# A list scheduler that reckons with a later landing of the compressed branch's first weights

## The chip, the cores and the metric

One core of a Trainium2 chip. The metric is the device time of one execution in microseconds (us), smaller is better. TensorE (PE) multiplies, VectorE (DVE) and ScalarE (ACT) do the elementwise work, GpSimd (POOL) a little of it, and SyncE (SP) issues all transfers from one queue.

## What is computed

A decoder layer on 512 tokens of width 1024 in float32. One normalised input goes through one projection into two attention mixers and their gates:

```python
h = rms_norm(x, norm_w[l])
proj = h @ w_in[l]
(q_a, k_a, v_a, z_a, q_b, kc, vc, ksl, vsl, kwn, vwn, gate_b, z_b, gate_m) = jnp.split(proj, split_points, axis=-1)
...
k_cmp = rms_norm(compress(heads(kc), cmp_pos_k[l], cmp_w1_k[l], cmp_w2_k[l]), k_norm_cmp[l])
v_cmp = compress(heads(vc), cmp_pos_v[l], cmp_w1_v[l], cmp_w2_v[l])
```

Mixer A (8 heads, "MoBA") and mixer B (8 heads, "NSA") are softmax attentions with a bias by distance. Mixer B has a third branch over compressed keys and values: `compress` takes windows of 32 tokens, 16 apart, adds a position term, and multiplies each window (2048 numbers) by a first weight (2048 x 256), applies gelu and multiplies by a second weight (256 x 64). Both mixers' outputs are gated with silu, projected to 1024, merged by sigmoid gates, projected once more and added to x.

## The kernel before, in words

**Products in pieces.** A float32 weight tile (128x512) is loaded into a raw buffer `wr`. ScalarE rounds it to the high part (`wh`, for the compressed branch `vh`), DVE subtracts that from the raw tile to get the low part (`wl`, `vl`), and PE multiplies both. The rounding is the cast of L402, the subtraction L412; the method that emits both is `Stream.split`. The raw buffers (`NRAW` = 6) are shared by all weights and come back first in, first out: the n-th load of a raw tile waits until the subtraction six raw tiles earlier is done. A stream of weights loads its next tile right behind the subtraction of an earlier one (`w.load`, called at the end of `split`'s chain).

**Two streams.** `W` holds the weights of the projections and of the end, in the trace `in_wtok`, `in_wchan` and `in_wbr`. `W1` holds the first weights of `compress`, in the trace `in_w`: 16 tiles, eight for K and then eight for V. `compress_h` takes them one by one: four matmuls per tile into `hps` (L940), two with the high part and two with the low part; after the eighth tile ScalarE copies `hps` to `hs` (L947), PE turns it round (`pu`, L952), and gelu and the second weight follow.

**Attention.** Per head: scores `sps` (PE, L1094), bias `T` and the maximum (DVE, L1114), exponential (ACT, L1125) and its factor (L1127, L1128), probabilities in two float16 halves `sb` (ACT L1132, DVE L1136), transposes of these from SP's queue (`dst`, L245), and the product with the values (`O`, PE, L1168). Two heads share one run of 24 such products; there are twelve runs, four for mixer A and eight for mixer B.

**What sets the order.** Every engine's instructions are put in order by a list scheduler that runs in the kernel's own Python. A piece of work is a `Chain`: steps with an engine and a cost in ns. Chains stand in a heap by the time at which their next step may begin; the step with the earliest time is emitted next on its engine, and `free[engine]`, the engine's time in the scheduler's books, moves on by its cost. PE's streams of work (scores, projections, compression, values) are generators that ask when their operand is ready and are taken by turns. A load's time comes from `dma` (L235): its issue, 1000 ns, the bytes and 1700 ns more. This landing time `t` is what a `split` chain starts with, if it is later than the scheduler's present time `now[0]`. Nothing on the chip reads these times; they decide only where an instruction stands in its engine's queue. An engine runs its queue in that order, and each instruction waits for its own operands.

Of the kernel before, what the change touches and what calls it, by code (L numbers as in the profile page):

```python
# [67 lines left out]
XQ = 1200  # L68
XW = 1700.0
XG = 400.0  # L70


QA, KA_, VA, ZA, QB, KC, VC, KSL, VSL, KWN, VWN, GB, ZB, GM = (
# [35 lines left out]
def hybrid_kernel(ctx: ExitStack, tc: tile.TileContext, x, x0, xT, wtok, wchan, gains, w1,  # L109
# [21 lines left out]
    now = [0.0]  # L131
# [14 lines left out]
    def ca(n):  # L146
        return 93 + 0.834 * n
# [13 lines left out]
    def either(n):  # L161
        return {"d": cd(n)}
# [173 lines left out]
    class Stream:  # L336
# [48 lines left out]
        def split(w, upto):  # L385
            for i in range(w.next, min(upto, len(w.tiles))):
                w.next = i + 1
                if isinstance(w.tiles[i], Sum):
                    if i not in w.chain:
                        w.split_sum(i)  # L390
                    continue
                while i not in w.raw:
                    w.load()
                w.ahead -= 1
                n, *squares = w.tiles[i][1:]
                (raw, t), hi, lo = w.raw.pop(i), w.mk_hi()[:, :n], w.mk_lo()[:, :n]
                w.out[i] = hi, lo
                c = w.chain[i] = Chain(max(now[0], t))

                def f(e, hi=hi, raw=raw):  # L400
                    if e is nc.scalar:
                        e.copy(hi, raw)  # L402
                    else:
                        e.tensor_scalar(hi, raw, 1.0, 1.0, op0=ALU.mult, op1=ALU.mult)
                c.do({"D": 205 + 0.54 * n} if w.first and not i else {"A": ca(n)}, f).mark((w, 0, i))
                if squares:
                    d = Chain(held=True)
                    c.call(lambda c=c, d=d: d.start(c.t))
                for o, m, g, acc, fn in squares:
                    d.do({"A": 190 + 0.834 * m}, lambda e, z=hi[:, o:o + m], y=R.bitcast(mybir.dt.bfloat16)[:, :m] if m > 256 else junk, g=g, acc=acc: e.activation(  # L410
                        y, z.bitcast(F32), AF.Square, scale=g, accum_out=acc)).call(lambda fn=fn, d=d: fn(d.t))
                c.do(either(n), lambda e, hi=hi, lo=lo, raw=raw: e.tensor_sub(lo, raw, hi.bitcast(F32))).mark((w, 1, i))  # L412
                c.call(w.load)
# [85 lines left out]
    def att(name, dt=F32R):  # L499
        return ap_.tile([P, 512], dt, name=nm(name), tag="a")  # L500
# [49 lines left out]
    def x_rms():  # L550
# [5 lines left out]
        for t in range(NT):  # L556
            nc.tensor.matmul(ps[:, t:t + 1], sq_sum[:, t * P:(t + 1) * P], ones, start=True, stop=True)
            yield 214
            if t < NT - 1:
                ready = now[0] + XG  # L560
                yield lambda: ready
# [98 lines left out]
    W1 = Stream([(w1[kv, q], 512) for kv in range(2) for q in range(8)], 2, lambda: att("vh"), lambda: att("vl"))  # L660
# [238 lines left out]
    def compress_w(kv):  # L899
        st = xws[kv] = []  # L900
        b = {}

        def emit(ps):
            ch = Chain(now[0] + 230)
            for g in range(2):
                for l in range(2):
                    v = lambda z, g=g, l=l: z[g * 64:(g + 1) * 64, :].rearrange("p (j l) -> p l j", l=2)[:, l, :]

                    def f(e, g=g, l=l, v=v):
                        if not g and not l:  # L910
                            b["X"] = alloc("gmt", "X", (P, 2, 256))
                        e.tensor_mul(b["X"][64 * l:64 * l + 64, g, :], v(ps), v(R))  # L912
                    ch.do({"D": 335}, f, ps if g and l else None, None if g or l else "gmt")
            for i8 in range(2):
                XW = att("XW", F32).rearrange("p (i g c) -> p i g c", g=2, c=C32)
                ch.do({"p": 140}, lambda e, XW=XW: e.memset(XW[:, :, :, 31:32], 0.0))
                for g in range(2):
                    ch.do({"d": 550}, lambda e, XW=XW, g=g, i8=i8: e.tensor_tensor(
                        XW[:, :, g, 0:31], b["X"][:, g, :].rearrange("p (c i) -> p i c", i=8)[:, :, i8:i8 + 31],
                        pos[:, kv, 8 * i8:8 * i8 + 8].unsqueeze(2).to_broadcast([P, 8, 31]), op=ALU.add),  # L920
                        (lambda: b["X"]) if i8 and g else None)
                for q in range(2):
                    xs = att("xs")
                    split(ch, xs.rearrange("p (i s c) -> p i s c", s=2, c=64),
                          XW[:, 4 * q:4 * q + 4].rearrange("p i g c -> p i (g c)"))
                    st.extend(xs[:, i * P:(i + 1) * P] for i in range(4))
            ch.mark(f"xw{kv}")
        yield from gemm_chan("kc" if not kv else "vc", emit)
# [75 lines left out]
    def compress_v2(G):  # L1004
        yield room("t")
        ps = psum("t", "pv2")
        for g in range(2):
            for a in range(2):
                nc.tensor.matmul(ps[:, g * 64:(g + 1) * 64], G[:, 2 * a + g].rearrange("p r c -> p (r c)"),
                                 w2t[:, 1, a, :], start=(a == 0), stop=(a == 1))  # L1010
        yield 600
        release(G)
        yield room("nraw")
        vr = alloc("nraw", "vr", (P, 2, DH))
        yield room("nraw")
        vh = alloc("nraw", "vh", (P, 2, 2, DH), F32R)
        vt = att("vz").rearrange("p (g s i d) -> p g s i d", g=2, s=2, i=2)
        vz.extend(vt[:, g] for g in range(2))
        ch = Chain(now[0] + 230)
        ch.do({"D": 200}, lambda e: e.tensor_scalar_mul(vr, ps[:, :P].rearrange("p (g d) -> p g d", g=2), 0.5), ps)  # L1020
        split(ch, vh, vr, vr)
        for g in range(2):
            ch.do({"D": 335}, lambda e, g=g: e.tensor_mul(
                vz[g], vh[:, g].bitcast(F32).unsqueeze(2).to_broadcast([P, 2, 2, DH]),
                hmask.unsqueeze(1).unsqueeze(3).to_broadcast([P, 2, 2, DH])), vh if g else None)
        ch.mark("cmpv")
# [721 lines left out]
```

## Time and profile before

| | |
|---|---|
| median of 3 timed runs | 422.29 us (421.83 to 422.44) |
| the profiled execution | 422.54 us |
| its span in the trace | 420.5 us |
| granted TensorE clock | 1.00 |
| busy: PE, DVE, ACT, POOL | 98%, 85%, 71%, 8% |

A row of a timeline gives the start in us, the duration, the engine, the line, the operation, output<-inputs, the shape and how many; the bracket at its end is the time that the engine stood idle just before, and what ended that. A row of the waits gives who waited, for whom, the total in us, how many times, and the longest. A row of the chain gives a start, a duration and what stood on the chain of work that ended last. Names have their buffer numbers left out.

### The profile page before, as it was taken

Reading aid. Unit: us, or ns where it says so; the run is one execution under the profiler, and the core shown is the slowest. Engines: PE = TensorE matmul, PEld = TensorE weight load, DVE = VectorE, ACT = ScalarE, POOL = GpSimd, SP = SyncE. Lnnn points to the kernel's source line nnn. Section 1 sums busy time; section 2 is a strip of 40 time slices with the busy share of each in tenths; the row PEclk is TensorE's granted clock in tenths of the full one; section 3 lists DMA queues with packets and bytes.
Section 4 is the critical chain, followed back from the end, with each engine's and each line's share of the span. In section 5 each row is a group of like instructions: output and inputs, shape, how many; then the busy total and the mean of one; then the engine's idle time right before and its main releaser. Section 6 shows DMA issues by size and latency. Waiting matters only on the chain.

```text
span 420.5 us, 7307 instructions
## 1 busy us (share of the span) xinstructions
PE 411.8 (98%) x2235; PEld 322.0 (77%) x2235; DVE 356.3 (85%) x933; ACT 297.9 (71%) x793; POOL 35.1 (8%) x37
## 2 busy tenths in 40 slices
PE   9999998999998999999999999999999999999996
PEld 7877875778976677897766777666777888888885
DVE  5967969999899987778999997899956967698993
ACT  7996748997797988727988897898943433445620
POOL 0015100123210033200000000000000000000000
PEclk9999999999999999999999999999999999999999
DMA  8951785688969988750878778889799597251232
GB/s 278 311 190 49 129 271 140 137 183 214 264 201 232 195 163 194 218 153 12 147 168 196 150 161 200 167 195 160 145 162 348 175 374 278 79 180 44 56 143 100
DMA packets 116693, 75.30 MB, mean 179 GB/s; under 512 B 89072, under 2 KB 92016, under 8 KB 116656
## 3 DMA queue, kind: packets, MB, share of 16 engines
q1 hardware_dynamic: 116656, 74.86, 70.5%
q8 instruction: 17, 0.28, 0.3%
q14 instruction: 20, 0.16, 0.1%
HBM read 51.11 MB, written 2.75 MB: 128 GB/s over the span
## 4 chain that ended last, share of the span: by engine, by line
PE 54%; DVE 23%; DMA 9%; ACT 5%; issue 5%; SPq 1%; POOL 1%; DVEq 0%; ACTq 0%; POOLq 0%
PE pgc L437 21%; PE pbr L437 9%; PE po L437 9%; PE pgt L437 8%; DMA wr<-in_wtok 5%; DVE sb L1114 4%; DVE wl L412 4%; DVE sb L1136 4%; DMA wr<-in_w 3%; PE O L1168 3%; PE sps L1094 3%; ACT wh L402 2%; DVE vl L412 1%; SPq L238 1%; DMA T<-rtab 1%
## 5 line engine op out<-in xcount | busy, mean ns | idle before, releaser
L437 PE MATMUL pgc<-hh,wh 128*128 128x512 f32 x208 | 87.1, 419 | 0.0
L412 DVE TENSOR_TENSOR wl<-wr,wh 128x512 fp32r<-128x512 f32 (+1 forms) x112 | 73.1, 669 | 11.8 <-ACT wh L402 11.6
L437 PE MATMUL pgc<-hh,wl 128*128 128x512 f32 x208 | 81.5, 392 | 0.0
L437 PE MATMUL pgc<-hl,wh 128*128 128x512 f32 x208 | 81.2, 390 | 0.0
L402 ACT CAST wh<-wr 128x512 fp32r<-128x512 f32 (+1 forms) x111 | 64.0, 599 | 11.2 <-DMA wr<-in_wtok 5.6
L1125 ACT ACTIVATE sb<-sb,sst 128x256 f32<-128x256 f32 (+3 forms) x96 | 53.2, 554 | 10.5 <-DVE sst L1114 10.2
L437 PE MATMUL pgt<-wh,hh 128*128 128x512 f32 (+2 forms) x160 | 58.3, 364 | 0.1
L437 PE MATMUL pgt<-wl,hh 128*128 128x512 f32 (+2 forms) x160 | 56.1, 351 | 0.5 <-DVE wl L412 0.4
L437 PE MATMUL pgt<-wh,hl 128*128 128x512 f32 (+2 forms) x160 | 55.8, 349 | 0.0
L1136 DVE SCALAR_TENSOR_TENSOR sb<-sb,sst 128x256 f16<-128x256 f32 (+3 forms) x96 | 51.1, 542 | 4.2 <-ACT sb L1132 3.9
L1114 DVE CUSTOM_DVE_ANT_0 sb<-sps,T,gst 128x512 f32<-128x512 f32 (+3 forms) x96 | 51.2, 541 | 3.5 <-PE sps L1094 1.6
L1132 ACT ACTIVATE sb<-sb,sst 128x256 f16<-128x256 f32 (+3 forms) x96 | 51.4, 552 | 4.0 <-DVE sst L1128 3.7
L437 PEld LDWEIGHTS pgc<-hh,wh 128*128 128x128 f32 x208 | 39.1, 188 | 8.6 <-issue 0.3
L437 PEld LDWEIGHTS pgc<-hh,wl 128*128 128x128 f32 x208 | 39.0, 188 | 8.6
L437 PEld LDWEIGHTS pgc<-hl,wh 128*128 128x128 f32 x208 | 39.2, 189 | 6.5
L1094 PE MATMUL sps<-qkt,qkt 128*128 128x512 f16 (+3 forms) x176 | 38.2, 310 | 1.6 <-DVE sst L1114 1.4
L489 POOL TENSOR_TENSOR nr<-nss,mhalf 128x8 f32<-128x8 f32 (+1 forms) x16 | 29.0, 1819 | 109.4 <-DVE nss L488 47.9
L437 PEld LDWEIGHTS pgt<-wl,hh 128*128 128x128 f32 x160 | 30.1, 188 | 5.5 <-DVE wl L412 1.6
L437 PEld LDWEIGHTS pgt<-wh,hh 128*128 128x128 f32 x160 | 30.2, 189 | 4.3 <-DVE X L912 0.4
L437 PEld LDWEIGHTS pgt<-wh,hl 128*128 128x128 f32 x160 | 30.2, 189 | 3.4
L1094 PEld LDWEIGHTS <-qkt 128*128 128x128 f16 x176 | 11.5, 98 | 21.4 <-issue 18.5
L437 PE MATMUL pbr<-yh,wh 128*128 128x512 f32 x64 | 26.4, 413 | 0.0
(229 smaller groups left out, 746.3 us busy)
## 6 DMA issues: line engine op xcount, KB each, us to landing
wr<-in_wchan SPq DMA_DIRECT2D x52, 256.0 KB, 3.8
wr<-in_wtok SPq DMA_DIRECT2D x36, 256.0 KB, 4.0
wq<-in_wout SPq DMA_DIRECT2D x36, 256.0 KB, 3.1
T<-rtab SPq DMA_DIRECT2D x16, 256.0 KB, 4.0
wr<-in_w SPq DMA_DIRECT2D x16, 256.0 KB, 3.7
wr<-in_wbr SPq DMA_DIRECT2D x16, 256.0 KB, 3.1
xr<-in_x SPq DMA_DIRECT2D x8, 256.0 KB, 5.3
x<-in_xT SPq DMA_DIRECT2D x7, 256.0 KB, 5.8
```

What stands on the lines that cost most here:

```text
L238: nc.sync.dma_start(out=dst, in_=src)
L402: e.copy(hi, raw)
L412: c.do(either(n), lambda e, hi=hi, lo=lo, raw=raw: e.tensor_sub(lo, raw, hi.bitcast(F32))).mark((w, 1, i))
L437: nc.tensor.matmul(dst, sts[i][a], mvs[i][b], start=(start and i == a == b == 0), stop=(stop and i == n - 1 and (a, b) == passes[-1]), ski ...
L489: c.do({"p": 700 + 150 * w}, lambda e: e.tensor_tensor(v(dst), v(ss), mhalf[:parts, :w], op=ALU.pow))
L1094: nc.tensor.matmul(sps[:, :n].rearrange("p (t n) -> p t n", n=P), qs, k4[:, x, j, :b + 1], start=not x, stop=bool(x))
L1114: e.tensor_tensor_reduce(z["sb"], sps[:, :L], T[:, S - L:], scale=nrunscale, scalar=3e38, op0=ALU.add, op1=ALU.min, accum_out=st[:, 0, b:b ...
L1125: c.do({"A": 279 + 0.834 * L}, lambda e: e.activation(z["sb"], z["sb"], AF.Exp, bias=st[:, 0, b:b + 1], scale=-1.0, accum_out=st[:, 1, b:b ...
L1132: e.activation(z["pp"][:, :L], z["sb"], AF.Copy, scale=s_)
L1136: c.do({"d": 59 + cd(L)}, lambda e: e.scalar_tensor_tensor(z["pp"][:, L:], z["sb"], s_, z["pp"][:, :L], op0=ALU.mult, op1=ALU.subtract))
L1168: nc.tensor.matmul(out, v[r][kb][:, vi * DH:(vi + 1) * DH], u.moving(kb, pi), start=p.first and kb == vi == pi == 0, stop=p.last and kb == ...
```

## The change

The landing time with which a `split` chain of the stream `W1` starts is put 1000 ns later. The other stream's chains, all costs, buffers and instructions stay as they are. Line numbers behind the new constant are one higher afterwards.

```diff
 XQ = 1200
 XW = 1700.0
 XG = 400.0
+LAND1 = 1000
...
                 n, *squares = w.tiles[i][1:]
                 (raw, t), hi, lo = w.raw.pop(i), w.mk_hi()[:, :n], w.mk_lo()[:, :n]
                 w.out[i] = hi, lo
-                c = w.chain[i] = Chain(max(now[0], t))
+                c = w.chain[i] = Chain(max(now[0], t + (LAND1 if w is W1 else 0)))
```

Counts and kinds of instructions are the same on every engine. PE's order is the same up to about 94 us of the trace and after the last run of attention products apart from what is shown below; between them it differs in many places.

ScalarE, round the copy of K's finished hidden sums `hs`. `vh_1736<-wr_1719` is the cast of V's first tile, `vh_1703` (not shown) that of K's last; `wh` are casts of other weights, `sb` and `sst` belong to the attention, `kb` to its keys. Before:

```order
L402 CAST vh_1736<-wr_1719 128x512
L1125 ACTIVATE sb_1771,sst_1723<-sb_1771,sst_1723 128x256
L1127 ACTIVATE sst_1723<-sst_1723 128x1
L1365 ACTIVATE th_1817<-zs_1660 128x512
L1132 ACTIVATE sb_1676<-sb_1676,sst_1580 128x128
L1125 ACTIVATE sb_1789,sst_1723<-sb_1789,sst_1723 128x128
L1127 ACTIVATE sst_1723<-sst_1723 128x1
L1132 ACTIVATE sb_1730<-sb_1730,sst_1723 128x512
L1033 COPY kb_1550<-kb_1550 128x2x64
L1127 ACTIVATE sst_1723<-sst_1723 128x1
L947 COPY hs_1853<-hps_1130 128x256
```

The same place now, where V's first tile is `vh_1818<-wr_1809`:

```order
L1034 COPY kb_1541<-kb_1541 128x2x64
L1128 ACTIVATE sst_1717<-sst_1717 128x1
L804 CAST kb_1542<-nraw_1559 128x2x64
L948 COPY hs_1863<-hps_1130 128x256
L403 CAST wh_1871<-wr_1663 128x512
L403 CAST wh_1873<-wr_1679 128x512
L403 CAST wh_1875<-wr_1690 128x512
L403 CAST wh_1877<-wr_1708 128x512
L1034 CAST kb_1542<-nraw_1559 128x2x64
L1200 CAST yh_1840<-zs_1654 128x512
L403 CAST vh_1818<-wr_1809 128x512
```

The cast of V's first tile stood ten rows ahead of the copy and stands seven rows behind it. The cast of K's last tile, which stood sixteen rows ahead of the copy, is now twelve rows ahead.

SyncE, the loads of the same tiles. `in_w` are first weights, `in_wtok` other weights, `rtab` the bias, `qkt` and `dst` transposes of the attention's keys and probabilities. Before, from K's last tile (`wr_1697`) on:

```order
L238 DMA wr_1697<-in_w 128x512
L238 DMA wr_1706<-in_wtok 128x512
L245 DMA_TRANSPOSE qkt_1438<-kb_1431 128x8x128
L238 DMA wr_1719<-in_w 128x512
L238 DMA T_1721<-rtab 128x1x512
L238 DMA wr_1742<-in_wtok 128x512
L245 DMA_TRANSPOSE dst_1794<-sb_1585 128x8x128
L245 DMA_TRANSPOSE dst_1794<-sb_1597 128x6x128
```

Now, where K's last tile is `wr_1721` and V's first `wr_1809`:

```order
L239 DMA wr_1690<-in_wtok 128x512
L239 DMA wr_1708<-in_wtok 128x512
L239 DMA T_1715<-rtab 128x1x512
L239 DMA wr_1721<-in_w 128x512
L246 DMA_TRANSPOSE qkt_1431<-kb_1424 128x8x128
L246 DMA_TRANSPOSE dst_1735<-sb_1575 128x8x128
L246 DMA_TRANSPOSE dst_1735<-sb_1587 128x6x128
L239 DMA wr_1809<-in_w 128x512
```

Both loads have moved back; V's first is behind two transposes of probabilities that it stood ahead of.

TensorE, the end of the last run of attention products (L1168, now L1169). `ch` and `vz` are the compressed branch's probabilities and values, `pgc` a projection with the weights `wh` and `wl`, `pbr` the branches' projection. Before:

```order
L1168 LDWEIGHTS vb_2457
L1168 MATMUL O_4200<-dst_4110,vb_2457 64x384
L1304 MATMUL O_4200<-ch_3257,vz_2519 128x512 x2
L437 MATMUL pbr_4331<-yh_3258,wh_4249 128x512
L437 MATMUL pbr_4331<-yl_3259,wh_4249 128x512
```

Now:

```order
L1169 LDWEIGHTS vb_2438
L1169 MATMUL O_4186<-dst_4091,vb_2438 64x384
L1305 MATMUL O_4186<-ch_3337,vz_2558 128x512 x2
L438 MATMUL pgc_4260<-hh,wh_4243 128x512
L438 MATMUL pgc_4260<-hl,wh_4243 128x512
L438 MATMUL pgc_4260<-hh,wl_4244 128x512
```

Twelve matmuls of a `pgc`, of which the first three are shown, ran ahead of this last run and now stand behind it, in front of the `pbr`.

## The prediction, made before the changed kernel ran

> **What bounds the kernel now.** I read the page first, then the windows of 10 us, the waits, the timelines round the largest pauses of TensorE, and the chain. The profiled execution took 422.54 us, 420.5 of it inside the span; 2.0 us lie around the span, and the median of the three timed runs, 422.29, is 0.25 below it, so a change of the span is carried over to the median as it is. The page's totals and its chain:
>
> ```profile
> PE 411.8 (98%) x2235; PEld 322.0 (77%) x2235; DVE 356.3 (85%) x933; ACT 297.9 (71%) x793; POOL 35.1 (8%) x37
> PE 54%; DVE 23%; DMA 9%; ACT 5%; issue 5%; SPq 1%; POOL 1%; DVEq 0%; ACTq 0%; POOLq 0%
> ```
>
> TensorE (PE) works nearly all the time. The change removes no instruction, so it can only win TensorE's pauses. Busy time by stretch (sum of the stretch, then PE, PEld, DVE, ACT, POOL, clock, DMA share, GB/s) shows where they are:
>
> ```profile
> 120.00:130.00 10.00, 10.00 (x52) 7.65 (x51) 10.00 (x33) 7.66 (x23) 0.00 (x0) 1.00 0.97 244
> 130.00:140.00 10.00, 8.53 (x43) 6.22 (x42) 9.63 (x28) 9.78 (x30) 1.01 (x1) 1.00 1.10 223
> 140.00:150.00 10.00, 9.21 (x62) 6.79 (x61) 9.24 (x35) 9.66 (x34) 0.76 (x1) 1.00 0.90 194
> 170.00:180.00 10.00, 9.83 (x74) 9.24 (x73) 8.44 (x23) 6.37 (x17) 2.57 (x2) 1.00 0.69 196
> 220.00:230.00 10.00, 10.00 (x66) 6.97 (x65) 10.00 (x31) 8.64 (x28) 0.00 (x0) 1.00 0.84 168
> 240.00:250.00 10.00, 9.77 (x46) 7.11 (x45) 9.16 (x31) 10.00 (x30) 0.00 (x0) 1.00 0.75 161
> 250.00:300.00 50.00, 50.00 (x299) 34.86 (x298) 44.24 (x139) 44.32 (x132) 0.00 (x0) 1.00 0.85 177
> ```
>
> PE lacks 1.5 us in 130 to 140 and 0.8 in 140 to 150, hardly anything elsewhere, at the full clock. The waits that bear on the change (total, times, longest):
>
> ```profile
> ACT vh L402 <- DMA wr<-in_w: 3.8, 5, 2.3
> DVE vl L412 <- ACT vh L402: 2.5, 5, 0.9
> PE pu L952 <- ACT hs L947: 1.3, 1, 1.3
> PE O L1168 <- DMA dst<-sb: 0.8, 1, 0.8
> PE hps L940 <- DVE vl L412: 0.2, 1, 0.2
> ```
>
> ScalarE (ACT) waits five times for a first weight, 3.8 us in all. The longest one, in ACT's timeline (start, duration, and in brackets the idle time before):
>
> ```profile
> 127.58 0.29 ACT L1033 CAST kb<-nraw 128x128 f16<-128x128 f32 x1
> 130.22 0.62 ACT L402 CAST vh<-wr 128x512 fp32r<-128x512 f32 x1 [2.34 <-DMA wr<-in_w]
> 130.74 0.50 ACT L1125 ACTIVATE sb<-sb,sst 128x256 f32<-128x256 f32 x1
> ...
> 133.53 0.35 ACT L947 COPY hs<-hps 128x256 f32<-128x256 f32 x1
> ```
>
> and TensorE's, for the two pauses:
>
> ```profile
> 132.22 0.40 PE L437 MATMUL pgt<-wl,hh 128*128 128x512 f32 x1
> 133.94 0.66 PE L952 MATMUL pu<-cst,hs 128*128 128x64 f32 x4 [1.32 <-ACT hs L947]
> ...
> 146.34 0.40 PE L437 MATMUL pgt<-wl,hh 128*128 128x512 f32 x1
> 146.67 0.40 PE L1168 MATMUL O<-dst,v 128*64 128x512 f16 x1
> 147.86 1.66 PE L1168 MATMUL O<-dst,v 128*64 128x512 f16 x22 [0.79 <-DMA dst<-sb]
> ...
> 156.94 0.51 PE L940 MATMUL hps<-vh,xs 128*128 128x256 f32 x2
> ```
>
> The cast at 130.22 rounds the first V tile, whose product PE takes up at 156.94, 26 us later. Yet ACT stands in front of it for 2.34 us, and behind it in the queue is the copy of `hs` (K's finished hidden sums) for which PE waits. The matmul of 132.22 should have been followed 0.23 us later (twelve take 2.73 below), so this pause costs 1.5 us; the third attention product (`O`, at 146.67) loses 1.1 in the same way, waiting for a transpose. The chain between them, and what later rows I need:
>
> ```profile
> 125.56 4.64 DMA wr<-in_w
> 130.22 0.63 ACT vh L402
> 145.11 2.71 DMA dst<-sb
> 147.86 1.66 PE O L1168 x19
> 168.47 3.65 DMA wr<-in_w
> 172.13 0.63 ACT vh L402
> 172.78 0.70 DVE vl L412
> 243.47 2.73 PE pgc L437 x12
> ```
>
> **The change part by part.** One number moves the assumed landing of each first weight 1.0 us back; all else is what the list scheduler makes of it.
>
> *The V tile's cast goes behind the copy of hs.* Ten rows ahead of it before, seven behind it now. The 2.34 us no longer stand in front of the copy. What does is K's last tile: its cast, then eleven rows of the same forms as those that ran between 130.22 and 133.53 (3.3 us for ten), which I put at 3.2 us, so the copy starts 3.8 us after that cast starts and is done 0.35 later. On PE's side the cast (0.63) and the subtraction (0.70) come before K's last product, and from there to `pu` the order holds 2.1 us of products: PE arrives 3.5 us after the cast starts, the copy ends at 4.2. So 0.7 of the 1.5 stay: **-0.8**. Bounds: all of it goes (-1.5), or nothing (0), where ACT now waits as long at K's last tile.
>
> *The third attention product.* It now has six more products ahead of it (1.4 us by 2.73 for twelve), and the probabilities that its transposes read come from the ACT queue that stood still. A pause of 1.1 under a cover of 1.4: **-1.1**. Without this cover, if the transposes come later too, 0.
>
> *V's last tile.* 0.3 us of PE (0.2 on the product, the rest on its weight load) goes with the chain of 168.47; the product now has 4 us more work ahead of it: **-0.3**.
>
> *New waits.* K's fourth and last tile are loaded and rounded later in the order; the raw buffers come back first in, first out, so the last tile's load starts when the subtraction six loads earlier is done. A load takes 3.7 us (median) to 4.64:
>
> ```profile
> wr<-in_w SPq DMA_DIRECT2D x16, 256.0 KB, 3.7
> ```
>
> plus the cast's 0.63, and DVE has only about 3.8 us of other work between these two subtractions. DVE then stands for 0.5 to 1.5 us, and PE has two groups of products in hand: I take **+0.3**, bounds 0 and 1.2. [...]
>
> These four give PE 1.9 us by about 180 us.
>
> *What PE is given and has to give back.* From 250 on PE has no pause, so 1.9 us is the gain unless a later product is late. The order puts the last attention product earlier: twelve matmuls that ran ahead of it (2.73 us) now run after it. SyncE's queue (SP) feeds it with transposes, and is full. The last of them in SP's timeline, their landing (count, median from issue), and the product:
>
> ```profile
> 242.51 1.05 SPq L238 DMA_DIRECT2D wr<-in_wchan  x2
> 245.10 9.75 SPq L245 DMA_TRANSPOSE dst<-sb  x7
> ...
> 305.34 8.86 SPq L245 DMA_TRANSPOSE dst<-sb  x6
> ```
>
> ```profile
> dst<-sb SPq DMA_TRANSPOSE x2, 3.0
> ```
>
> ```profile
> 316.43 1.82 PE L1168 MATMUL O<-dst,vb 128*64 128x512 f16 x24
> ```
>
> The last transpose was issued at 313.0 and landed at 316.0: 0.4 us of slack, 0.6 with the first product that doesn't need it. PE would now be there 1.9 + 2.7 = 4.6 us earlier. If the transposes come s earlier, PE waits 4.0 - s. Bounds: s = 4 (SP had gaps ahead of 245.10, the last of them 1.5 us, so its queue can follow), wait 0; s = 0 (DVE is full at 220 to 230 and sets when probabilities come), wait 4.0, the whole gain and 2.1 more. I take s = 2.9: the 1.9 that PE's products for this stage come earlier, and 1.0, an estimate, for a subtraction (0.7) and a few small steps that stand behind, no longer ahead of, the probabilities that filled SP's queue at 245.10. Wait: **+1.1**.
>
> Sum: -0.8 - 1.1 - 0.3 + 0.3 + 1.1 = -0.8 us, so 422.54 becomes 421.7 and the median **421.5**. A measurement of this kernel can tell about 0.2% (0.84 us) from no change, so this case lies on the line between the two.
>
> **The rivals.**
>
> *The transposes don't follow (slower).* At the last attention product everything depends on s; the end moves by 2.1 - s (never below -1.9), so it decides at s = 2.1. For: the chain of the selection scores now has a gate of channel `zs` ahead of it in DVE, which waits for a later PE product, DVE has no idle time at 220 to 230, and SP has none from 245 to 314, so nothing lost before 245 is won back. Against: ahead of these probabilities DVE has less to do, not more. With s between 0 and 1.2 the end is 0.9 to 2.1 later: 423.2 to 424.4, middle **423.8**.
>
> *The wait only changes its place.* ACT waits at K's last tile, whose load now starts late, as long as it did at V's first (2.3), and DVE and PE with it; or the changed loads leave PE's pauses as long in other rows. For: five waits on these loads existed, and a cast further back also loads its successor later, since the next load is started after the subtraction. Against: the one that cost most was a tile not yet needed. PE then keeps -0.3 of the three gains, and the end is **422.0** to 422.5.
>
> *The change doesn't do what it says:* the loads of these weights are issued further back too (two of them now stand behind transposes of 1.2 us each, as the 4.64 us load did), so the casts wait as before. It ends like the rival before, and is counted with it.
>
> *All of it is gained.* The transposes follow fully (s = 4): -1.9, or **420.4**.
>
> **How the numbers follow.** Forecast case (s between 2.1 and 4, end 420.4 to 422.3) 0.54, of which 0.34 lies beyond 0.84 us faster; all gained, with the pause at `hs` gone too, 0.08; the wait moves 0.16, 0.10 of it within 0.2% and 0.06 of it slower (new waits at K's tiles at their upper bound, with nothing gained at 147); the transposes don't follow 0.22, of which 0.20 is over the line. So faster 0.42, same 0.32, slower 0.26. The range runs from 420.2 (all gained and 0.2 more of the pause at `hs`) to 423.6 (s = 0.4); the forecast case alone is 420.4 to 422.3.
>
> **What would show it.** Right: ACT's 2.34 us wait is gone, `hs` is copied within 4 us of the cast of K's last tile and PE's pause at `pu` is 0.5 to 1.0; no pause at the third attention product; a pause of about 1 us at the last one or two of them, with `dst` as what ended it. Wrong: PE pauses by over 2 us in the sum of the last attention products (slower rival), or ACT still waits over 2 us on a first weight ahead of `hs` (the wait moved), or PE's 250 to 300 has a pause of another kind.

## The result, and the profile after

The changed kernel is slower. Eleven executions of each gave a median of 427.0 us against 422.24, a ratio of 1.0111 (95% interval 1.009 to 1.0133). One execution of each (430.44 and 452.72) fell in a slower state and is left out of the ratio, here and below. Its profiled execution took 424.81 us with a span of 422.8, 2.3 more than the 420.5 of before. The page's totals, after:

```profile
PE 412.7 (98%) x2235; PEld 323.3 (76%) x2235; DVE 355.5 (84%) x929; ACT 297.4 (70%) x797; POOL 34.5 (8%) x37
```

TensorE still works nearly all the time, so the 2.3 us must be pauses. The windows of the changed kernel show where (columns as in the prediction: sum, PE, PEld, DVE, ACT, POOL, clock, DMA share, GB/s):

```profile
130.00:140.00 10.00, 9.23 (x45) 6.77 (x44) 9.39 (x24) 10.00 (x31) 0.00 (x0) 1.00 1.00 204
140.00:150.00 10.00, 10.00 (x66) 7.12 (x65) 9.93 (x40) 10.00 (x35) 1.74 (x1) 1.00 1.04 223
160.00:170.00 10.00, 9.63 (x61) 7.03 (x61) 5.58 (x12) 7.63 (x22) 1.47 (x2) 1.00 0.95 216
170.00:180.00 10.00, 9.69 (x78) 9.35 (x78) 8.01 (x17) 6.17 (x13) 1.71 (x2) 1.00 0.88 244
220.00:230.00 10.00, 9.34 (x60) 6.55 (x57) 10.00 (x28) 8.57 (x23) 0.00 (x0) 1.00 1.10 160
260.00:270.00 10.00, 7.69 (x52) 5.33 (x51) 7.89 (x22) 8.02 (x24) 0.00 (x0) 1.00 0.84 175
```

The two pauses that the prediction set out from have shrunk: 130 to 140 lacks 0.77 us instead of 1.47, 140 to 150 nothing instead of 0.79. Three new ones stand behind them: 0.7 us in 160 to 180, where before had 0.2, 0.7 in 220 to 230 and 2.3 in 260 to 270, where before had none. The waits name them:

```profile
ACT vh L403 <- DMA wr<-in_w: 2.8, 1, 2.8
PE sps L1095 <- DVE sst L1115: 2.1, 3, 1.1
PE O L1169 <- DMA dst<-sb: 2.0, 1, 2.0
```

ScalarE waits once for a first weight instead of five times. PE's one wait for a transpose, 0.8 us at the third run of attention products before, is now 2.0 us, and it stands elsewhere:

```profile
134.14 0.66 PE L953 MATMUL pu<-cst,hs 128*128 128x64 f32 x4 [0.58 <-ACT hs L948]
147.75 1.94 PE L1169 MATMUL O<-dst,v 128*64 128x512 f16 x23
169.71 0.51 PE L941 MATMUL hps<-vl,xs 128*128 128x256 f32 x2 [0.22 <-DVE vl L413]
172.07 0.50 PE L941 MATMUL hps<-vl,xs 128*128 128x256 f32 x2 [0.31 <-DVE vl L413]
227.16 0.48 PE L1095 MATMUL sps<-qkt,qkt 128*128 128x384 f16 x2 [0.66 <-DVE sst L1115]
...
262.43 0.39 PE L1093 MATMUL sps<-qkt,qkt 128*128 128x256 f16 x2
264.83 1.89 PE L1169 MATMUL O<-dst,vb 128*64 128x512 f16 x24 [2.00 <-DMA dst<-sb]
```

The row of 264.83 is the eighth of the twelve attention runs. The twelfth, at 316.24, has no wait.

**Why the eighth.** The order puts it nine products (2.0 us) further forward than before, and its last transpose comes later. SyncE's queue, in before (the seven transposes ahead of these rows, from 245.10 on, stand in the prediction) and then in the changed kernel:

```profile
254.90 0.57 SPq L238 DMA_DIRECT2D wr<-in_wbr  x1
255.57 0.55 SPq L238 DMA_DIRECT2D T<-rtab  x1
256.17 0.58 SPq L238 DMA_DIRECT2D wr<-in_wchan  x1
256.84 1.23 SPq L245 DMA_TRANSPOSE dst<-sb  x1
258.12 0.57 SPq L238 DMA_DIRECT2D wr<-in_wchan  x1
258.80 6.46 SPq L245 DMA_TRANSPOSE dst<-sb  x5
```

```profile
245.67 4.49 SPq L246 DMA_TRANSPOSE dst<-sb  x3
250.21 0.57 SPq L239 DMA_DIRECT2D wr<-in_wchan  x1
250.88 5.22 SPq L246 DMA_TRANSPOSE dst<-sb  x4
256.15 0.57 SPq L239 DMA_DIRECT2D wr<-in_wbr  x1
256.82 0.55 SPq L239 DMA_DIRECT2D T<-rtab  x1
257.46 1.22 SPq L246 DMA_TRANSPOSE dst<-sb  x1
258.74 1.04 SPq L239 DMA_DIRECT2D wr<-in_wchan  x2
259.89 6.58 SPq L246 DMA_TRANSPOSE dst<-sb  x5
```

and the changed kernel's chain:

```profile
261.23 3.56 DMA dst<-sb
```

The eighth run needs the second of the last five. It was issued at 260.1 (258.80 and a fifth of 6.46) and is now issued at 261.23, 1.1 later; it landed 3.0 after its issue, at 263.15, and now 3.56 after it, at 264.8. Before, the product stood at 264.53 with 1.4 us to spare; now PE is there at 262.8 and waits.

What this transpose moves had long been ready. DVE finished the probabilities at 256.08 in before and at 256.31 now, with this row:

```profile
255.96 0.35 DVE L1137 SCALAR_TENSOR_TENSOR sb<-sb,sst 128x128 f16<-128x128 f32 x1
```

So the transpose stood behind others in SyncE's queue for 4.9 us. The rows above follow each other with at most 0.1 us between them, from 245.67 on (245.10 in before), with nine transposes ahead of this one in both kernels, but five loads where before had four. Of the 1.1 us that it is issued later, 0.6 is the later start of this full stretch (the first transpose of it waits for DVE, which finished its probabilities at 245.60 against 245.04) and 0.5 the load more.

**Where VectorE lost time.** VectorE in two windows, before and after:

```profile
160.00:200.00 40.00, 39.83 (x270) 33.72 (x270) 31.51 (x81) 25.75 (x68) 6.22 (x3) 1.00 0.55 145
200.00:250.00 50.00, 49.71 (x288) 35.26 (x286) 48.90 (x154) 45.38 (x134) 0.00 (x0) 1.00 0.82 167
```

```profile
160.00:200.00 40.00, 39.32 (x265) 32.87 (x265) 28.15 (x73) 22.94 (x60) 3.17 (x3) 1.00 0.57 147
200.00:250.00 50.00, 49.34 (x287) 35.59 (x286) 50.00 (x156) 46.49 (x136) 0.00 (x0) 1.00 0.84 159
```

DVE does 3.4 us less in 160 to 200 (28.15 against 31.51) and is then full to the last tenth for 50 us, so it can't catch up. It is idle in good part because the later V tiles hold up the scores of the compressed branch (`scp`), which need V's result by the rule of their generator; their first addition, and a later row, before and after:

```profile
185.78 0.49 DVE L1257 TENSOR_TENSOR sc<-scp,cst 128x128 f32<-128x128 f32 x2 [0.58 <-PE scp L1252]
...
193.22 0.66 DVE L1366 TENSOR_TENSOR zs<-pgc,R 128x512 f32<-128x512 f32 x1
```

```profile
189.01 0.49 DVE L1258 TENSOR_TENSOR sc<-scp,cst 128x128 f32<-128x128 f32 x2 [1.63 <-PE scp L1253]
...
193.15 0.68 DVE L1367 TENSOR_TENSOR zs<-pgc,R 128x512 f32<-128x512 f32 x1
```

The addition comes 3.2 us later; the gate of channel `zs`, of which the prediction's slower rival spoke, doesn't. A DVE that is behind shows in the 0.66 us that PE waits at 227.16 for a maximum, and in the 0.6 us by which the full stretch of SyncE's queue starts later. That this lateness comes from the idle time in 160 to 200 is a reading, which the experiments put to a test. None of them changes SyncE's queue alone.

### The profile page after: what moved, and what is told of

It is laid out like the page before. It is cut to its first block, busy times and chain, and to the rows that moved or that the text cites. A ratio compares the mean times of both kernels' runs of the same rounds, so it can differ in the third digit from the quotient of the medians.

```text
span 422.8 us, 7307 instructions
## 1 busy us (share of the span) xinstructions
PE 412.7 (98%) x2235; PEld 323.3 (76%) x2235; DVE 355.5 (84%) x929; ACT 297.4 (70%) x797; POOL 34.5 (8%) x37
## 4 chain that ended last, share of the span: by engine, by line
PE 65%; DVE 19%; DMA 6%; issue 4%; ACT 4%; SPq 0%; DVEq 0%; ACTq 0%
PE pgc L438 18%; PE pgt L438 17%; PE po L438 9%; PE pbr L438 8%; PE pgf L700 6%; DVE sb L1115 5%; DVE sb L1137 3%; PE O L1169 3%; DVE wl L413 3%; PE sps L1095 2%; DMA wr<-in_wtok 2%; ACT wh L403 1%; DMA wr<-in_w 1%; DMA wr<-in_wchan 1%; DMA T<-rtab 1%
## 5 line engine op out<-in xcount | busy, mean ns | idle before, releaser
L1133 ACT ACTIVATE sb<-sb,sst 128x256 f16<-128x256 f32 (+3 forms) x96 | 50.5, 552 | 4.6 <-DVE sst L1129 4.3
L1095 PE MATMUL sps<-qkt,qkt 128*128 128x512 f16 (+3 forms) x176 | 37.3, 310 | 2.1 <-DVE sst L1115 2.1
L490 POOL TENSOR_TENSOR nr<-nss,mhalf 128x8 f32<-128x8 f32 (+1 forms) x16 | 26.8, 1679 | 110.2 <-DVE nss L489 66.8
```

The costliest lines, as they stand in the source:

```text
L490: c.do({"p": 700 + 150 * w}, lambda e: e.tensor_tensor(v(dst), v(ss), mhalf[:parts, :w], op=ALU.pow))
L1095: nc.tensor.matmul(sps[:, :n].rearrange("p (t n) -> p t n", n=P), qs, k4[:, x, j, :b + 1], start=not x, stop=bool(x))
L1133: e.activation(z["pp"][:, :L], z["sb"], AF.Copy, scale=s_)
```

## The experiments

Fifteen more runs were made: the first four in the text below on the second chip, the next four on another, and those from the sizes of the constant on, with the third copy of the changed kernel, on the third. All times are us; the ratio is to the kernel before on the same chip, as it is on record, which is not always the quotient of the two medians.

| kernel | median | ratio | interval |
|---|---|---|---|
| the changed kernel, second chip | 425.48 | 1.0112 | 1.0089 to 1.0134 |
| the changed kernel, third chip | 424.36 | 1.0078 | 1.0052 to 1.0103 |
| before, again | 421.7 | 1.0003 | 0.9986 to 1.0019 |
| V's tiles only | 422.12 | 1.002 | 0.9999 to 1.0041 |
| K's tiles only | 424.0 | 1.0071 | 1.0043 to 1.0098 |
| after, eighth run later | 423.65 | 1.0072 | 1.0047 to 1.0097 |
| after, scores freed from V | 423.85 | 1.0054 | 1.0032 to 1.0075 |
| before, scores freed from V | 422.92 | 1.0038 | 1.0017 to 1.0058 |
| before, scores late | 423.85 | 1.0049 | 1.0025 to 1.0073 |
| constant -500 | 426.96 | 1.0129 | 1.01 to 1.0158 |
| constant 300 | 426.15 | 1.0099 | 1.0075 to 1.0123 |
| constant 500 | 423.66 | 1.0048 | 1.003 to 1.0066 |
| constant 700 | 421.41 | 0.9987 | 0.9971 to 1.0004 |
| after, pause filled | 426.41 | 1.0114 | 1.0086 to 1.0141 |
| constant 300, pause filled | 426.89 | 1.0139 | 1.0109 to 1.0168 |

To compare profiles I counted PE's lost time between the attention runs: the time from the start of one run to the start of another, less the products in between, each form taken at the distance to the next product that it had in before's trace (the 40th percentile). Only differences between kernels mean something. "Start" ends with the first run, at about 84 us, and has the same order in all; "early" is first to fourth run, up to about 163 us; "V" is fourth to seventh, "eighth" seventh to eighth, "late" all behind it.

| kernel | start | early | V | eighth | late |
|---|---|---|---|---|---|
| before | 6.55 | 11.40 | 12.04 | 2.76 | 12.66 |
| before, again | 6.64 | 11.63 | 11.99 | 2.67 | 12.67 |
| after | 6.36 | 10.42 | 13.22 | 5.09 | 12.61 |
| after, second chip | 6.45 | 10.15 | 13.39 | 5.47 | 12.61 |
| after, third chip | 5.99 | 10.19 | 12.72 | 5.78 | 13.83 |
| V's tiles only | 6.02 | 11.32 | 12.13 | 2.47 | 13.33 |
| K's tiles only | 7.44 | 11.46 | 12.48 | 2.60 | 13.23 |
| after, eighth run later | 7.11 | 10.24 | 13.88 | 4.79 | 12.84 |
| after, scores freed | 6.91 | 11.38 | 11.78 | 2.67 | 14.18 |
| before, scores freed | 6.97 | 11.24 | 11.47 | 2.47 | 14.74 |
| before, scores late | 5.97 | 9.51 | 13.13 | 2.87 | 12.68 |
| constant -500 | 6.82 | 12.23 | 13.20 | 4.59 | 12.62 |
| constant 300 | 6.43 | 10.58 | 13.02 | 5.35 | 14.21 |
| constant 500 | 7.40 | 12.45 | 11.39 | 3.10 | 12.67 |
| constant 700 | 7.84 | 9.76 | 12.24 | 2.59 | 13.26 |

The "start" column shows how far one profile can be trusted: with one order it runs from 5.97 to 7.84. Early, the order of before stands in four rows (before, again, scores freed, scores late): 9.51 to 11.63, mean 10.95; that of the changed kernel in five (after, three times, eighth run later, scores freed): 10.15 to 11.38, mean 10.48. So the early gain is some 0.5 us, up to 1.2 against the first profile of before. The stretch from the fourth to the seventh run takes 0.7 to 1.4 back: in the changed kernel's profile the brackets in it are 0.15, 0.22 and 0.31 at V's tiles and 0.66 at 227.16, in that of before 0.17 at V's tiles and 0.29 at one score. The eighth run takes 2.3 to 3.0, and the stretch behind it nothing (in its 13.83 on the third chip the granted clock is 0.50 in 264 to 266, of which more below).

**The changed kernel again**, unchanged, on a second chip.

> The changed kernel once more, unchanged. The ratio of 1.011 is 4.7 us, while its one profile shows a span only 2.3 us longer. Theory A: a pause of TensorE of 2 to 2.5 us ahead of the eighth run of attention products sometimes lets the granted clock drop; runs whose mean clock is 1.000 take 424 to 425.5, runs at 0.992 to 0.998 take 1.5 to 4 us more, and the kernel before shows 1.000 throughout. Rival B: the longer runs have longer waits and the clock is a by-product of the chip; then the kernel before shows clocks under 1 just as often, and length and clock do not go together.

It was slower by the same ratio, 1.0112, and its eighth run waited at the same place:

```profile
265.20 1.89 PE L1169 MATMUL O<-dst,vb 128*64 128x512 f16 x24 [2.37 <-DMA dst<-sb]
```

So this wait is a property of the order, not of one execution.

**V's tiles only.**

```diff
-                c = w.chain[i] = Chain(max(now[0], t + (LAND1 if w is W1 else 0)))
+                c = w.chain[i] = Chain(max(now[0], t + (LAND1 if w is W1 and i >= 8 else 0)))
```

> The later landing is assumed for V's eight tiles alone; K's keep the old one. Forecast's theory: the wait of 2.3 us ahead of the copy of hs goes, and PE's pause at pu with it, since it was V's first tile that stood there; K's last tile does not wait longer. The eighth run of attention products has 243.3 us of products ahead of it instead of 242.9 before and 240.9 in the changed kernel, so it should not wait by 2 us: 421 to 422.5. Rival: the order of the later stage is off in any reshuffling and some run waits all the same: 424 or more.

It came within the line of before, 1.002. DVE has the same hole as in the changed kernel, 28.61 us of work in 160 to 200 against 28.15 there, and yet its eighth run loses nothing (2.47): its order has 243.3 us of products ahead of that run by the table's reckoning, against 240.9 in the changed kernel and 242.9 in before. Its last transpose for that run is issued at 259.55, with four loads ahead of it as in before. A late DVE alone does not make the wait.

**K's tiles only** (the same line with `i < 8`).

> The later landing is assumed for K's eight tiles alone. If the new waits in the stretch from 125 to 175 us (K's last tile 2.8 us, V's tiles 0.5 each) come from K's later loads, they are here too. The eighth run stands behind 241.6 us of products (242.9 before, 240.9 in the changed kernel): by theory A PE waits there for 1 to 2 us and the time is 423 to 425; if the loss belongs to V's tiles it is 422.

Slower by 1.0071, without the wait at the eighth run (2.60) and with as much lost early as in before (11.46), though not at the same places: it waits 0.59 us at `pu`, 0.27 at the third run, and 0.90 for a transpose of keys at 114.7, where before had no wait. By the table its profile loses 1.8 us more than before, half of it at the start, where the order is the same. The measured difference is 2.9 us, and its cause is not in this profile.

**The eighth run later.** The order alone is moved for one run:

```diff
-            yield need(*(("p", id(u), b) for u in p.us for b in range(NT)))
+            late = 3000 if p is pairs[7] else 0
+            ready = need(*(("p", id(u), b) for u in p.us for b in range(NT)))
+            yield lambda: None if ready() is None else ready() + late
```

> The changed kernel with one line more: the eighth run of attention products counts as ready 3.0 us later in the scheduler's books, so it stands behind 245.2 us of products instead of 240.9; the runs ahead of it keep their places, the last ones move by 0 to 2 us. Theory A (PE waits 2 us because this one run stands too early): the pause ahead of it goes, all clocks are 1.000 and the time is 422 to 423. Rival C (DVE is behind with everything from 240 on, so the wait goes on to the next run or to the scores): the pause appears at another place with 1.5 to 2.5 us and the time stays at 424 to 425 or more.

The wait at the run is gone, but in this profile not the loss, which stays at 4.79 in the stretch. The waits:

```profile
PE sps L1095 <- DVE sst L1115: 4.0, 5, 1.2
```

PE waits for the maxima of the scores instead, five times and 4.0 us (2.1 in three in the changed kernel); two of these waits, 0.26 and 1.18 us, stand at 262.7 and 265.2, just ahead of the run, which starts at 269.71. VectorE is behind, and with the run out of the way the next product that needs it waits. But the profiled execution, 425.99, is the slowest of six; four of the six took 423.3 to 423.9. The median, 423.65, is 1.8 us below that of the changed kernel on the same chip, 425.48, so moving this one run wins back about two fifths of the 4.4 us (the intervals of the two ratios just overlap), and no profile shows an execution in which it did.

**Before, again** (one blank line added).

> The kernel before, with one blank line more so that its lines carry the changed kernel's numbers: a second profile of it, on another chip. Both theories expect the ratio 1.000 and a time within 1 us of the kernel before. It tells how far one profile stands from another of the same order: the pauses at pu (1.5 us) and at the third run of attention products (1.1) should be there again, and DVE should do 31 to 32 us of work between 160 and 200.

No difference, 1.0003. But its profile, of the same order, differs from before's where the prediction had read its two largest terms:

```profile
133.75 0.66 PE L953 MATMUL pu<-cst,hs 128*128 128x64 f32 x4 [0.43 <-ACT hs L948]
148.22 1.66 PE L1169 MATMUL O<-dst,v 128*64 128x512 f16 x22 [0.59 <-DMA dst<-sb]
```

The pause at `pu` costs 0.6 us here and 1.5 in the first profile. Within one order these pauses come and go between executions.

**Before, with the compressed scores made late** by 5000 ns in the scheduler's books:

```diff
-            yield need("cmpk", "cmpv", ("qb", g))
+            ready = need("cmpk", "cmpv", ("qb", g))
+            yield lambda: None if ready() is None else ready() + (5000 if g == 0 else 0)
```

> The kernel before, with the compressed branch's scores alone counted as ready 5 us later in the scheduler's books: they stand behind 173.1 us of products instead of 167.5 (171.0 in the changed kernel), the loads and casts of the first weights and the runs of attention products keep their places. Theory D (what the change costs is that these scores come later, so that DVE stands idle ahead of them and, full from 200 to 250, stays late, and PE waits for it): 2 to 5 us slower, with less DVE work done by 200 and a wait of PE on DVE or on transposes between 225 and 300. Rival E (the cost is in the first weights' loads and in the places of the attention runs): within 0.5 us of the kernel before.

This gives before the hole in DVE and nothing else of the change, and it costs 1.0049 (2.1 us). In its profile (at 421.29 the fastest of its twelve executions) DVE has 29.12 in 160 to 200, and PE stands once more on its maxima:

```profile
237.40 0.38 PE L1095 MATMUL sps<-qkt,qkt 128*128 128x256 f16 x2 [1.48 <-DVE sst L1115]
```

Its eighth run stands behind as many products as in before and has no wait. Six of the twelve executions had a mean clock of 0.994 to 0.996 and took 423.73 to 425.33, with a median of 424.5; the six at 0.999 and 1.00 have a median of 422.2, 0.5 above before, and two of before's 29 executions on this chip were under 0.998. So a late DVE has a price of its own, but most of it is in the executions with the lower clock.

**The scores freed from V's result**, in the changed kernel and in before:

```diff
-            yield need("cmpk", "cmpv", ("qb", g))
+            yield need("cmpk", ("qb", g))
...
             def before(o, j=j):
+                yield need("cmpv")
```

> The changed kernel, with the compressed branch's scores no longer held back until V's chain is finished (they need K's side alone; V's is asked for where its values are used): they stand behind 162.5 us of products instead of 171.0. Theory D: DVE does its score chain before 190, is not late at 200, and the time falls to that of the kernel before or below, 419 to 422. Rival E: the waits for the first weights (2.8 us of ACT, 1 us of PE at V's tiles) are still there, and it stays at 424 or more.

> The same in the kernel before: its compressed scores stand behind 163.7 us of products instead of 167.5. Theory D: DVE gains a little (it waited 1.1 us for these scores), so 0 to 1.5 us faster than the kernel before; PE's early pauses of 1.5 and 1.1 stay. Rival E: no change.

In the changed kernel DVE's work is back (31.35 in 160 to 200) and the eighth run, at 262.91, has no wait. A new one stands behind it:

```profile
278.09 0.48 PE L1095 MATMUL sps<-qkt,qkt 128*128 128x384 f16 x2 [1.59 <-DVE sst L1115]
```

The ratio is 1.0054, about half of the loss (the changed kernel as it is did not run beside it; its three ratios are 1.0111, 1.0112 and 1.0078); the new wait at 278 is 1.59 us. The edit changes SyncE's queue as well: its full stretch starts at 244.86, with eight transposes and four loads ahead of the run's last one, so this run doesn't tell a late DVE from a fuller queue. In before the same edit, meant to let DVE start sooner, makes it slower, 1.0038. So "more work early for DVE is better" is too simple: an edit that moves the order has its own pauses wherever they fall (here 0.70 and 0.86 us at scores of 276.7 and 288.4).

**Other sizes of the constant.** Four values, of which two have, from about 180 us on, the order of the changed kernel (-500, 300), one the order of before (500), and one that of the K-only kernel (700):

```diff
-LAND1 = 1000
+LAND1 = 500
```

> The changed kernel with 500 ns in the place of 1000. Its order differs from the kernel before between about 94 and 160 us (K's and V's first weights are rounded further back, as in the changed kernel), and from there to the end it is the kernel before's order row by row. Theory L (the loss comes from the order that the schedule falls into behind 160 us, not from where the first weights are loaded and rounded): between 1 us faster and 0.5 us slower than the kernel before. Rival W (the loss comes from the first weights' later loads and casts): 2 us or more slower.

> The changed kernel with -500 ns: the first weights are assumed to land earlier than in the kernel before. From about 165 us on the order is the changed kernel's, row by row. Theory L: 3 to 5 us slower than the kernel before, with the pauses at V's tiles or the eighth run of attention products (2 us or more) as in the changed kernel, though no weight stands further back. Rival W: as the kernel before, 421 to 422.5.

> The changed kernel with 300 ns. The first weights' places move less than with 500, but from about 165 us on the order is the changed kernel's, row by row. Theory L: 3 to 5 us slower. Rival W: the cost grows with the number, so at most as slow as the kernel with 500, 421 to 423.

> The changed kernel with 700 ns. From about 165 us on the order is that of the kernel in which only K's tiles had the later landing (it took 1.0071 of the kernel before). Theory L: 1.005 to 1.009 again. Rival W: between the kernel with 500 and the changed kernel, whatever these turn out to be.

The longest early wait of -500, 2.09 us, stands at 137.73 and is for a maximum. The eighth run in -500 and in 300:

```profile
266.58 1.89 PE L1169 MATMUL O<-dst,vb 128*64 128x512 f16 x24 [1.96 <-DMA dst<-sb]
```

```profile
265.12 2.79 PE L1169 MATMUL O<-dst,vb 128*64 128x512 f16 x24 [2.19 <-DMA dst<-sb]
```

The two with the late order of the changed kernel wait 1.96 and 2.19 us and are slow (1.0129 and 1.0099), even where the constant has the other sign. The two without it, whose eighth runs start at 266.13 (500) and 262.85 (700), don't wait. This ties the wait to the late order, whatever made it. But 500, with before's late order, is still 1.0048, with 12.45 us lost early, and 700 shares its late order with the K-only kernel and is 0.9987 where that is 1.0071, with 9.76 against 11.46 lost early. By size the ratios run 1.0129, 1 (at zero), 1.0099, 1.0048, 0.9987, 1.0111: no trend. The constant picks an order; it doesn't shorten a wait in proportion. And 700 cannot be told from before.

**The pause filled.** In three comparisons the change cost 4.8, 4.4 and 2.7 us in the median, and the profiled executions of the first two differ from that of before by 2.3 and 2.7. In the profile at 300 the granted clock (the last column but two) falls to 0.50 behind that pause:

```profile
264.00:266.00 2.00, 0.88 (x12) 0.79 (x13) 0.92 (x6) 2.00 (x7) 0.00 (x0) 0.99 1.09 200
266.00:268.00 2.00, 2.00 (x19) 1.34 (x13) 1.21 (x5) 2.00 (x7) 0.00 (x0) 0.50 0.30 60
268.00:270.00 2.00, 2.00 (x6) 1.12 (x7) 0.90 (x2) 0.13 (x2) 0.00 (x0) 0.66 0.61 157
```

To see whether this is the rest, eight products of zeros were added to the sum of the eighth run ahead of its own, so that PE works while it waits:

```diff
+            if p is pairs[7]:
+                for _ in range(8):
+                    nc.tensor.matmul(o[:, :S], warm[:, :1].to_broadcast([P, P]), warm[:, :1].to_broadcast([P, S]),
+                                     start=False, stop=False, skip_group_check=True)
```

> The changed kernel with eight products of zeros (0.21 us each) added to the eighth run's sum just ahead of it, where PE stands idle for 2.2 us: every other engine's order is the same. Theory K (a pause of over 2 us sometimes halves the clock for 3.4 us, and the part of the 4.7 us that no profile at full clock shows is this): the wait for the transposes ends when it did, the median falls by 0.5 to 2.5 us to the level of the runs at full clock (424 to 425), with fewer runs under 0.998. Rival N (the clock plays no part): the same median as the changed kernel beside it.

> The changed kernel unchanged, on the same chip as the one with the filled pause. Theory K: 425 to 428, several of the runs with a mean clock of 0.992 to 0.998, and these longer by about 1.7 us for each 0.004. Rival N: no such relation.

> The kernel with 300 ns and the same eight products of zeros ahead of the eighth run; without them it took 1.0099 of the kernel before, and its profile shows the clock halved for 3.4 us right behind the pause. Theory K: 1.004 to 1.008. Rival N: 1.010 again.

The pause is filled (the changed kernel with the products):

```profile
265.24 1.69 PE L1166 MATMUL O<-warm 128*128 128x512 bf16 x7
267.19 1.89 PE L1173 MATMUL O<-dst,vb 128*64 128x512 f16 x24 [0.26 <-DMA dst<-sb]
```

It is not faster: 1.0114 against 1.0078 for the unchanged copy on the same chip, and at 300 it is 1.0139 against 1.0099. Four of the six executions of the filled kernel ran at a mean clock of 1.00 and took 425.6 to 426.81, where three of the copy's at 1.00 took 423.92 to 424.66; why it is slower at the full clock isn't shown. The copy's eighth run waits as in the other two profiles of its order:

```profile
264.42 3.11 PE L1169 MATMUL O<-dst,vb 128*64 128x512 f16 x24 [2.46 <-DMA dst<-sb]
```

With the products of zeros the clock stays at 1.00 behind the eighth run (264 to 272 of the changed kernel; at 300 the mean of 0.83 in 160 to 170 accounts for the 0.996 over the whole span). But in both profiles it falls elsewhere, behind waits of 1.79 and 1.99 us. In the first the clock is 0.50 in 172 to 174, 0.75 in 174 to 176 and 0.83 in the mean of 170 to 180, so it fell at about 171.6; in the second the products take 0.63 us instead of 0.39 to 0.40 from 162.06 on. That is some 0.8 us behind each wait, an estimate from these numbers:

```profile
170.83 0.50 PE L941 MATMUL hps<-vh,xs 128*128 128x256 f32 x2 [1.79 <-ACT vh L403]
```

```profile
161.24 0.27 PE L996 MATMUL pkt<-cst,kr 64*128 64x64 f32 x1 [1.99 <-DVE kr L992]
```

The idea that the halved clock behind the eighth run is the rest of the loss has fallen.

## Why the prediction was wrong, point by point

**What bounds the kernel: right.** PE's pauses decide, and the two at `pu` and the third run were moved as described. ACT's wait ahead of the copy became one at K's last tile, 2.80 us for a load of 4.33 us ahead of the cast at 129.92; the copy of `hs` started at 133.72, 3.8 us behind it, as worked out.

**The pause at `pu`, -0.8: right in its mechanism, sized on one execution.** 0.7 of the pause's cost was to stay; by the table's reckoning 0.75 stayed in the first profile of the changed kernel. But the 1.5 that it was taken off is near one end of what before's early order shows: the other three profiles have 0.6, 0.5 and 1.6. On another execution the gain is anything from nothing to 0.8.

**The third run, -1.1: the same.** No pause is left there. Where before's first profile has a bracket of 0.79, the other three of its order have 0.59, 0.26 and none. The two together gave some 0.5 in the mean and 1.2 at the most, not 1.9.

**V's last tile, -0.3: right for the tile, wrong for the stage.** The product of which it spoke (the seventh of V's eight, at 172.96 in before, at 176.72 now) no longer waits. But the fifth and sixth tile, which came at 166.44 and 167.61 without a wait, come at 168.98 and 171.34 with waits of 0.15, 0.22 and 0.31 us. The delay was reckoned for one tile where the change sets back eight.

**New waits at K's tiles, +0.3.** No new wait at these tiles is in the list; what is left at `pu` holds them.

**"What PE is given and has to give back": the step that failed.** It looked at the last attention run alone, the only one that its order rows show, and put a wait of 1.1 there, with the transposes 2.9 us earlier (s = 2.9). There is no wait (12.61 us against 12.66 lost behind the eighth run), and the transposes didn't come earlier: the full stretch of SyncE's queue that began at 245.10 begins at 245.67, and the last run's last transpose is issued at 312.79 instead of 313.0. The same two movements, a run put forward in PE's order and transposes that don't follow, stood at the eighth run, which has 2.0 us fewer products ahead of it and whose last transpose is issued 1.1 us later; PE waits 2.00, 2.37 and 2.46 us in the three profiles. The slower rival had the right argument in SyncE's queue, which has no gap and wins nothing back: the eighth run's last probabilities lie ready for 4.9 us while that queue issues others. Its other cause, the gate `zs` ahead of the selection scores in DVE, is not what the trace shows: the gate starts when it did. The compressed scores come 3.2 us later. The prediction held against this rival that "DVE has less to do, not more" there; it did 3.4 us less in 160 to 200, but by standing idle, and the probabilities that open SyncE's full stretch came 0.6 us later, not earlier.

Two figures in that step were off as well. The last transpose of before, issued at 313.0, landed 2.3 us later, at 315.3; 316.0 comes from the median of two. And by the step's own formula, 2.1 - s, the upper end of the range, 423.6, belongs to s = 0.8; s = 0.4 gives 424.0.

The rival's 423.2 to 424.4 was the right kind of end, at another run. With the runs' sizes the sum is -0.5 early, +0.7 to +1.4 from the fourth to the seventh run and +2.3 to +3.0 at the eighth: +2.5 to +3.9 where -0.8 was forecast.

**What stays open.** The medians differ by 4.8, 4.4 and 2.7 us in the three comparisons, the sum of the terms is 2.5 to 3.9. Part of the rest is in which executions were profiled. On the second chip the changed kernel's profile, 425.19, is near its median, 425.48, but the profile of before, 422.54, is 1.5 above before's median there, 421.07. In the first comparison it is the changed kernel's profile, 424.81, that lies 2.2 below its median, and seven of its eleven executions had a clock under 1.00. The pauses of one order differ from one execution to the next by about as much, so one profile per kernel cannot settle the remainder. Nor did a run move the one load more, or the start of SyncE's full stretch, by itself, and why the first probabilities of that stretch are 0.6 us later is argued from DVE's idle time and not shown.

## What to carry to other kernels

When a change moves a list schedule, go through every run of products that is fed by transposes, not the last one: compare for each how much work now stands ahead of it, how late its last operand is issued, and whether that operand waits for its data or, as here, for its turn in the queue that issues it. Size the pauses on several executions of before, since one order gave 0.5 to 1.6 us for the same pause. And a constant of such a scheduler is a choice among orders with a scatter of over 1%: its direction says little, and a gain in one stage is worth what the later stages leave of it.

## What the hardware showed that was not expected

In five profiles (the third copy of the changed kernel, -500, 300 and the two filled ones) the granted clock fell to 0.5 at a wait of PE of 1.79 to 2.46 us: once inside the wait, four times up to 0.9 us behind it. All five were taken on the third chip, but mean clocks of 0.992 to 0.996 stand on the others too, in the first comparison and in six of twelve executions of before with the scores late. In the rows of 300 above the pause ends at 265.12, and the clock is 0.50 in 266 to 268 and 0.66 in the next two microseconds. In the third copy's profile the wait ends at 264.42, and the clock has fallen before that:

```profile
262.00:264.00 2.00, 0.00 (x0) 0.00 (x0) 1.15 (x4) 2.00 (x7) 0.00 (x0) 0.90 0.82 160
264.00:266.00 2.00, 1.58 (x13) 1.13 (x14) 1.44 (x7) 2.00 (x5) 0.00 (x0) 0.50 0.75 146
266.00:268.00 2.00, 2.00 (x19) 1.43 (x15) 0.56 (x1) 1.15 (x6) 0.00 (x0) 0.75 0.58 165
```

A mean of 0.90 is 0.4 us at half speed, so it fell at about 263.6, 0.8 us before the wait ended. With 2.0 and 1.0 us in the next two rows that makes 3.4 us at 0.5. The windows of the other four lose as much: 0.99, 0.50 and 0.66 in 264 to 270 at 300, 0.56 and 0.59 in 138 to 142 at -500, and a mean of 0.83 over 10 us in the two filled ones. This costs up to 1.7 us of work each time, an estimate, half of the 3.4. It did not follow every such pause: the changed kernel's first two profiles waited 2.00 and 2.37 us at the eighth run, -500 waited 1.96 us there, and all three have a clock of 1.00 round it (260 to 270). In the first comparison the four executions of the changed kernel at a mean clock of 1.00 took 423.77 to 425.32 us, the others, at 0.992 to 0.998, 426.18 and more; 3.4 us at half speed in a span of 423 makes a mean of 0.996. Why the clock falls at one such wait and not at another is not shown by any run.
